# Attention scores of a hybrid decoder layer: fp32 products replaced by three fp32r products of split operands

## The chip, the cores and the metric

The kernel runs on one core of one Trainium2 chip. The metric is the time of one execution on the device in microseconds (us); lower is better. Times are medians of several runs. A profiled execution gives the trace, with the start and length of each instruction on each engine: PE is TensorE's products and PEld its weight loads, DVE is VectorE, ACT is ScalarE, POOL is GpSimd and SP issues the DMAs.

## The reference

One layer for 256 positions of width 2048. The input is normed, and one projection feeds three branches of width 1024. Each is gated by a SiLU, projected back to 2048, merged by sigmoid gates, projected once more, normed and added to the input:

```python
h = rms_norm(x, pre_g)
a_u, a_v, a_g, b_x, b_g, x_q, x_g, gate_logits = split(h @ w_in)
y_a = spatial_gating(a_u, a_v, ...) * silu(a_g)          # layer norm of a_v, causal mix of positions
y_b = s5_branch(b_x, ...) * silu(b_g)                     # complex diagonal scan, gelu, then a GLU
y_x = memory_cross_attention(x_q, rms_norm(mem), ...) * silu(x_g)
out = sum(sigmoid(gate_logits[n]) * (y_n @ w_branch[n])) @ w_out
return x + rms_norm(out, post_g)
```

The change touches the cross-attention: 4 heads of width 256, 256 queries, 256 memory keys.

```python
k = (mem_n @ w_k).reshape(bsz, n_mem, XA_HEADS, XA_HEAD_DIM)
scores = einsum('bshd,bmhd->bhsm', qh, k) * (XA_HEAD_DIM ** -0.5)
p = softmax(scores, axis=-1)
o = einsum('bhsm,bmhd->bshd', p, v)
```

## The kernel before, in words

All matrices are fp32. The large products are made as fp32r products of a high and a low part: `split_to` (L91) has ScalarE round a tile to fp32r (L92, the high part) and VectorE subtract that from the tile (L93, the low part). For a weight tile w and an input x, the kernel adds w_hi x_hi, w_hi x_lo and w_lo x_hi. `cm_mm` (L173 to L177) does so with channels on the partitions, by a product of 512 columns for w_hi (both parts of x side by side) and one of 256 for w_lo; `tm_mm` (L180 to L182) does it with positions on the partitions, by three products of 512 columns.

Weights come from HBM in tiles of 1 MB (`raw`, three buffers). Each is split in two halves, each half into one of four `hl` buffers. The products of one half are called a block here: eight pairs of `cm_mm` or twelve products of `tm_mm`, 2.6 us on TensorE either way. A split of weights may start when TensorE has finished the block four before it.

The stages follow each other on TensorE: `w_bx` (S5 input), `w_xq` (queries), `wk` and `wv` (keys and values of the memory), `w_xg`, gates and projection of the attention branch (`merge(2)`), `w_av`, `w_ag` (beside it the layer norm of a_v, L819 on), `w_au`, `merge(0)`, `w_bg`, the gates of branch B (`sgB`), the GLU of the S5 branch (`yg` against `glu`), its projection, `w_out`.

TensorE's instructions run in the order in which the program is written. Those of the other engines are put in order by a scheduler, by priority and by when their inputs should be there; splits of weights are given priority.

Small work is put between the blocks by hand-written generators. After each block `pump` is called with a credit (`rate`). It first steps each generator in the list `bg[2]` to its next `yield None`, and takes the numbers that they yield from the credit; what is left goes to the S5 work, `s5_main`, which stops when the credit is spent. The S5 work has 32 steps: a product `bu` (L560), multiplies by tables E, two scans (L599), multiplies again, sums `s`. After every fourth step one readout `y` (L624, eight products) follows, then a gelu (`s5_gelu`, L639 on): VectorE adds into U (L374), ScalarE squares (L643), VectorE does two steps (L368, L371), ScalarE takes a sigmoid (L647), VectorE multiplies into U (L371). The result is split (L92, L93) into `yg` (H2, H3), input of the GLU; its last part, the eighth, comes from the last readout.

Attention is four generators of this kind, `attn(h)`, started together at `w_xg`: head h first waits 4h blocks, then makes its scores (L711: two query blocks by two halves of the head, fp32, 256 columns each) in the single PSUM buffer `misc`, then the softmax, then transposes (L732) in a block each. `attn_out(h)` follows in `merge(2)`. The queries lie in slot X0 (`qT`), the keys in M0 (`kT`), the values in M1. Slots H0 to H3 held the normed memory until the end of `wv`; in `w_xg` H0 receives `sx` and H1 the transposed probabilities, and H2 and H3 receive `yX` once attention's output is made.

Of the kernel before, what the change touches and what calls it, by code (L numbers as in the profile page):

```python
# [10 lines left out]
F32R = mybir.dt.float32r  # L11
# [7 lines left out]
P = 128  # L19
# [24 lines left out]
def trunk(ctx: ExitStack, tc: tile.TileContext, I, out):  # L44
    nc = tc.nc
    v, a, g, pe = nc.vector, nc.scalar, nc.gpsimd, nc.tensor
# [18 lines left out]
    def nm(s):  # L65
        n_[0] += 1
        return f"{s}_{n_[0]}"

    def slot(tag, shape, dt=F32):
        return big.tile(shape, dt, tag=tag, name=nm(tag))  # L70

    def small(shape, dt=F32):
        s = nm("sm")
        return const.tile(shape, dt, tag=s, name=s)
# [16 lines left out]
    def split_to(hi, lo, src):  # L91
        a.copy(out=hi, in_=src)  # L92
        v.tensor_tensor(out=lo, in0=src, in1=hi.bitcast(F32), op=ALU.subtract)  # L93
# [38 lines left out]
    def in_order2(z):  # L132
        return z.rearrange("p i (b c) -> p i c b", c=2)
# [518 lines left out]
    qT = slot("X0", [P, 8, T])  # L652
# [16 lines left out]
    kT = slot("M0", [P, 8, T])  # L669
# [35 lines left out]
    def attn(h):  # L705
        for _ in range(4 * h):
            yield None
        sc = miscp.tile([P, 2, T], F32, tag="misc", name=nm("sc"))
        for qb in range(2):
            for c in range(2):  # L710
                pe.matmul(sc[:, qb, :], lhsT=qT[:, 2 * h + c, qb::2], rhs=kT[:, 2 * h + c, :],  # L711
                          start=c == 0, stop=c == 1)
        yield None
        nb = small([P, 2])
        sm = small([P, 2])
        v.tensor_reduce(out=nb, in_=sc, axis=AX.X, op=ALU.max)
        v.tensor_scalar(out=nb, in0=nb, scalar1=-1.0 / 16.0, scalar2=None, op0=ALU.mult)
        p = wk.tile([P, 2, T], F32, tag="w1", name=nm("p"))
        for qb in range(2):
            a.activation(out=p[:, qb, :], in_=sc[:, qb, :], func=AF.Exp, scale=1.0 / 16.0, bias=nb[:, qb:qb + 1],  # L720
                         accum_out=sm[:, qb:qb + 1])
        yield 0.7
        yield None
        v.reciprocal(out=sm, in_=sm)
        for qb in range(2):
            v.tensor_scalar(out=p[:, qb, :], in0=p[:, qb, :], scalar1=sm[:, qb:qb + 1], scalar2=None, op0=ALU.mult)
        yield 0.6
        yield None
        tp = miscp.tile([P, 2, T], F32, tag="misc", name=nm("tp"))
        for mb in range(2):  # L730
            for qb in range(2):
                pe.transpose(tp[:, mb, qb * P:(qb + 1) * P], p[:, qb, mb::2], ident)  # L732
        yield None
        a.copy(out=pT[:, h], in_=tp)

    def attn_out(h):
        for _ in range(h):
            yield None
        po = miscp.tile([P, 2, T], F32, tag="misc", name=nm("po"))
        for c in range(2):  # L740
            for mb in range(2):
                pe.matmul(po[:, c, :], lhsT=vv[:, mb, (2 * h + c) * P:(2 * h + c + 1) * P], rhs=pT[:, h, mb, :],
                          start=mb == 0, stop=mb == 1)
        yield None
        o = wk.tile([P, 2, T], F32, tag="w1", name=nm("o"))
        t = o.rearrange("p i (c b) -> p i c b", c=2)
        d = in_order2(sx[:, 2 * h:2 * h + 2, :])
        a.activation(out=t, in_=d, func=AF.Sigmoid)
        v.tensor_tensor(out=d, in0=po.rearrange("p i (c b) -> p i c b", c=2), in1=d, op=ALU.mult)
        yield 0.6  # L750
        v.tensor_tensor(out=t, in0=d, in1=t, op=ALU.mult)
        yield 0.6
        t = o
        d = yX[h // 2][:, 2 * (h % 2):2 * (h % 2) + 2]
        split_to(d[:, :, 0], d[:, :, 1], t)
        yield 1.2
# [3 lines left out]

    rate["cm"] = RT[2]
    bg[2].extend(attn(h) for h in range(4))
    cm_pairs(I["w_xg"], 8, xhl, evac_xg)
    bg[2].extend(attn_out(h) for h in range(4))

    mg = None
# [19 lines left out]
    def csl(c):  # L786
        return slice(c * 512, (c + 1) * 512)
# [116 lines left out]
    for bp in range(4):  # L904
# [9 lines left out]
        b = slice(2 * bp, 2 * bp + 2)  # L914
        v.tensor_tensor(out=t, in0=t, in1=u[:, b, :], op=ALU.mult)
        v.tensor_tensor(out=t, in0=t, in1=sb[:, b, :], op=ALU.mult)
        for i in range(2):
            d = yB[2 * bp + i]
# [25 lines left out]
    for c in range(4):  # L944
# [3 lines left out]
        for tb in range(2):  # L948
            d = sgB[tb][:, csl(c)]
# [68 lines left out]
    for tb in range(2):  # L1018
# [3 lines left out]
        c = slice(tb, tb + 1)  # L1022
# [107 lines left out]
```

## Time and profile before

| | |
|---|---|
| median of 3 runs | 917.3 us (917.0 to 917.46) |
| span of the profiled execution, first to last instruction | 915.4 us |
| instructions | 12965 |
| granted TensorE clock, mean | 0.998 of full |
| DMA read from HBM | 190.39 MB, 210 GB/s over the span |
| busy in 180 to 190 us (first scores) | PE 10.00, DVE 8.02, ACT 7.60 of 10 us |
| busy in 210 to 220 us | PE 10.00, DVE 6.59, ACT 4.37 of 10 us |

The time of a run is a little above the span, which leaves out what lies ahead of the first and behind the last instruction. In a row of the order of time the columns are: start in us from the span's start, length in us, engine, line, operation, output<-inputs, partitions x elements, xcount where equal rows are merged, and in brackets how long the engine had stood idle and what ended that. In a row of waits: who waited for whom, us in total, times, the longest. In a row of one line's instructions, three lengths in ns are the least, the median and the greatest. A product's length includes its way through the array, so neighbours overlap: what it costs is the distance between starts.

### The profile page before, as it was taken

To read this page: it belongs to the slowest core of one execution; us is meant where nothing else is said; L and a number is where in the kernel's file an instruction comes from. 1 tells how busy PE (TensorE), PEld (TensorE's weight loads), DVE (VectorE), ACT (ScalarE), POOL (GpSimd) and SP (SyncE) were. 2 spreads that over 40 slices of the span, in tenths; PEclk is the share of its full clock that TensorE was granted. 3 is DMA by queue.
4 is the path that set the end of the run, shared out by engine and by line. 5 is a ranking of instruction groups with operands and counts; after the bars stand their busy time and mean duration, and the time that the engine had idled before them with its cause. 6 is when DMAs were issued, how large, how long until landed. Compare 5 with 4: busy or idle time off the path is not lost. (4 is left out here: it accounts for less than half of the span.)

```text
span 915.4 us, 12965 instructions
## 1 busy us (share of the span) xinstructions
PE 902.2 (99%) x4864; PEld 797.8 (87%) x4864; DVE 779.5 (85%) x1329; ACT 535.0 (58%) x866; POOL 22.2 (2%) x46
## 2 busy tenths in 40 slices
PE   8999999999999999999999999999999999999996
PEld 6999898899888888888899888888988888998896
DVE  7899957986789999999877999999998977876554
ACT  7576655665456576565545656756655646544452
POOL 1000000000000000000000000000000000000000
PEclk9999999999999999999999999999999999999999
DMA  9888655556355556555655555555665456657542
GB/s 343 325 304 301 218 214 194 190 192 228 138 190 193 197 197 241 214 184 200 247 184 184 190 185 193 203 193 198 227 216 213 174 208 228 218 185 276 192 176 92
DMA packets 30175, 193.33 MB, mean 211 GB/s; under 512 B 3744, under 2 KB 4128, under 8 KB 8352
## 3 DMA queue, kind: packets, MB, share of 16 engines
q1 hardware_dynamic: 28000, 186.08, 56.9%
q0 software_dynamic: 1536, 4.20, 1.4%
q10 hardware_dynamic: 576, 2.23, 0.6%
q8 instruction: 38, 0.62, 0.3%
q14 instruction: 25, 0.20, 0.1%
HBM read 190.39 MB, written 2.10 MB: 210 GB/s over the span
## 5 line engine op out<-in xcount | busy, mean ns | idle before, releaser
L93 DVE TENSOR_TENSOR hl<-raw,hl 128x1024 fp32r<-128x1024 f32 x319 | 388.5, 1221 | 97.3 <-ACT hl L92 93.8
L92 ACT CAST hl<-raw 128x1024 fp32r<-128x1024 f32 x319 | 330.2, 1045 | 182.5 <-PE acc L182 109.8
L175 PE MATMUL acc<-x,hl 128*128 128x512 f32 x736 | 241.1, 382 | 0.2 <-DVE x L169 0.2
L174 PE MATMUL acc<-x,hl 128*128 128x256 f32 x690 | 189.7, 275 | 2.1 <-DVE hl L93 1.8
L181 PE MATMUL acc<-hl,x 128*128 128x512 f32 x448 | 170.4, 380 | 1.1 <-DVE hl L93 1.0
L180 PE MATMUL acc<-hl,x 128*128 128x512 f32 x448 | 171.3, 382 | 0.0
L182 PE MATMUL acc<-hl,x 128*128 128x512 f32 x448 | 169.8, 379 | 0.0
L175 PEld LDWEIGHTS acc<-x,hl 128*128 128x128 f32 x736 | 136.7, 189 | 17.5 <-ACT hl L92 0.7
L174 PEld LDWEIGHTS acc<-x,hl 128*128 128x128 f32 x690 | 132.3, 192 | 4.9 <-DVE hl L93 3.6
L181 PEld LDWEIGHTS acc<-hl,x 128*128 128x128 f32 x448 | 84.7, 189 | 14.2 <-DVE hl L93 3.0
L180 PEld LDWEIGHTS acc<-hl,x 128*128 128x128 f32 x448 | 84.7, 189 | 13.8 <-issue 2.5
L182 PEld LDWEIGHTS acc<-hl,x 128*128 128x128 f32 x448 | 84.7, 189 | 11.8
L180 PE MATMUL acc<-hl,H 128*128 128x512 f32 (+1 forms) x224 | 83.6, 373 | 0.0
L181 PE MATMUL acc<-hl,H 128*128 128x512 f32 (+1 forms) x224 | 83.2, 372 | 0.0
L182 PE MATMUL acc<-hl,H 128*128 128x512 f32 (+1 forms) x224 | 83.2, 372 | 0.0
L175 PE MATMUL acc<-H,hl 128*128 128x512 f32 x192 | 62.8, 383 | 0.1
L174 PE MATMUL acc<-H,hl 128*128 128x256 f32 x176 | 48.3, 275 | 0.4 <-ACT H L92 0.4
L180 PEld LDWEIGHTS acc<-hl,H 128*128 128x128 f32 x224 | 42.4, 189 | 5.6 <-issue 0.4
L182 PEld LDWEIGHTS acc<-hl,H 128*128 128x128 f32 x224 | 42.4, 189 | 5.6
L181 PEld LDWEIGHTS acc<-hl,H 128*128 128x128 f32 x224 | 42.4, 189 | 5.3
L371 DVE TENSOR_TENSOR p<-p,E 128x512 f32<-128x512 f32 x64 | 44.1, 689 | 1.0
L599 DVE TENSOR_TENSOR_SCAN p<-s5r,p 128x256 f32<-128x256 f32 x64 | 42.5, 683 | 0.9
(248 smaller groups left out, 1166.4 us busy)
## 6 DMA issues: line engine op xcount, KB each, us to landing
raw<-w_gate SPq DMA_DIRECT2D x48, 1024.0 KB, 4.7
raw<-w_br SPq DMA_DIRECT2D x24, 1024.0 KB, 4.7
raw<-w_out SPq DMA_DIRECT2D x16, 1024.0 KB, 4.8
raw<-w_xq SPq DMA_DIRECT2D x8, 1024.0 KB, 5.0
raw<-wk SPq DMA_DIRECT2D x8, 1024.0 KB, 4.7
raw<-wv SPq DMA_DIRECT2D x8, 1024.0 KB, 4.8
raw<-w_xg SPq DMA_DIRECT2D x8, 1024.0 KB, 4.7
raw<-w_av SPq DMA_DIRECT2D x8, 1024.0 KB, 4.8
```

The source lines that it names most:

```text
L92: a.copy(out=hi, in_=src)
L93: v.tensor_tensor(out=lo, in0=src, in1=hi.bitcast(F32), op=ALU.subtract)
L174: pe.matmul(ps[:, 0:T], lhsT=wl, rhs=hl.moving(0), start=False, stop=False)
L175: pe.matmul(ps, lhsT=wh, rhs=hl.moving_both(), start=first, stop=last)
L180: pe.matmul(ps, lhsT=hl.stationary(0, tb), rhs=two(wh), start=first, stop=False)
L181: pe.matmul(ps, lhsT=hl.stationary(0, tb), rhs=two(wl), start=False, stop=False)
L182: pe.matmul(ps, lhsT=hl.stationary(1, tb), rhs=two(wh), start=False, stop=last)
L371: v.tensor_tensor(out=o, in0=i0, in1=i1, op=op)
L599: v.tensor_tensor_scan(out=p2[:, ri], data0=rb, data1=p1[:, ri], initial=0.0, op0=ALU.mult, op1=ALU.add)
```

## The change

Each head now first splits its queries and its keys into high and low parts, in the same way as weights, in slot H2 (heads 0 and 2) or H3 (heads 1 and 3). The split also puts even and odd columns apart. Each split yields 0.6 of credit, as other work of VectorE does. Two blocks later the scores are made: for each query block and each half of the head the products high x high, high x low and low x high, each of 256 columns, twelve a head for the four of before. As the rest of attention is then two blocks later, `attn_out` waits two blocks longer. Lines behind the scores have numbers greater by 8 in the changed kernel.

```diff
     def attn(h):
         for _ in range(4 * h):
             yield None
+        qk = slot(f"H{2 + h % 2}", [P, 2, 2, 2, 2, P], F32R)
+        for i, f in enumerate((qT, kT)):
+            d = f[:, 2 * h:2 * h + 2].rearrange("p k (b c) -> p k c b", c=2)
+            split_to(qk[:, i, :, :, 0], qk[:, i, :, :, 1], d)
+            yield 0.6
+        yield None
+        yield None
         sc = miscp.tile([P, 2, T], F32, tag="misc", name=nm("sc"))
         for qb in range(2):
             for c in range(2):
-                pe.matmul(sc[:, qb, :], lhsT=qT[:, 2 * h + c, qb::2], rhs=kT[:, 2 * h + c, :],
-                          start=c == 0, stop=c == 1)
+                q_, k_ = qk[:, 0, c], Pairs(qk[:, 1, c])
+                for i, (x_, y_) in enumerate(((0, 0), (0, 1), (1, 0))):
+                    pe.matmul(sc[:, qb, :], lhsT=q_[:, qb, x_], rhs=k_.moving(y_), start=c + i == 0, stop=c == 1 and i == 2)
         yield None
...
     def attn_out(h):
-        for _ in range(h):
+        for _ in range(h + 2):
             yield None
```

Three places show how the order moves. VectorE before, from the weights of block 2 of `w_xg` (hl_1912) to those of block 3 (hl_1940); p and E are an S5 step's:

```order
L93 TENSOR_TENSOR hl_1912<-raw_1884,hl_1912 128x1024
L599 SCALAR_TENSOR_TENSOR p_190_1870<-s5r,p_189_1869 128x256
L374 SCALAR_TENSOR_TENSOR E_1867<-E_1867,pwr,t_2349 128x64 x2
L371 TENSOR_TENSOR p_189_1869<-p_190_1870,E_1766 128x512
L371 TENSOR_TENSOR p_190_1870<-p_190_1870,E_1766 128x512
L93 TENSOR_TENSOR hl_1940<-raw_1938,hl_1940 128x1024
```

The same place now (hl_1910, hl_1931; H_199 is head 0's tile of splits, X its queries, M its keys):

```order
L93 TENSOR_TENSOR hl_1910<-raw_1884,hl_1910 128x1024
L93 TENSOR_TENSOR H_199_1905<-X_38_548,H_199_1905 128x4x128
L93 TENSOR_TENSOR H_199_1905<-M_80_1017,H_199_1905 128x4x128
L599 SCALAR_TENSOR_TENSOR p_190_1870<-s5r,p_189_1869 128x256
L374 SCALAR_TENSOR_TENSOR E_1867<-E_1867,pwr,t_2572 128x64
L93 TENSOR_TENSOR hl_1931<-raw_1929,hl_1931 128x1024
L374 SCALAR_TENSOR_TENSOR E_1867<-E_1867,pwr,t_2572 128x64
L371 TENSOR_TENSOR p_189_1869<-p_190_1870,E_1766 128x512
L371 TENSOR_TENSOR p_190_1870<-p_190_1870,E_1766 128x512
```

The head's two subtractions have come in, and the S5 multiplies and one step of E have moved behind block 3's weights. VectorE before, at the start of the layer norm beside `w_ag` (BN_STATS; hl_4031 and hl_4061 are weights of blocks 4 and 5 of `w_ag`). The scan L599 and p are an S5 step's, whose two multiplies by E and two sums s stand further down:

```order
L93 TENSOR_TENSOR hl_4031<-raw_4008,hl_4031 128x1024
L827 BN_STATS sm_3967<-H_443_3539 128x6
L827 BN_STATS sm_4123<-H_443_3539 128x6
L829 BN_AGGR sm_3968<-sm_3967 128x2
L599 SCALAR_TENSOR_TENSOR p_567_4444<-s5r,p_566_4443 128x256
L831 TENSOR_SCALAR sm_3972<-sm_3968 128x1
L93 TENSOR_TENSOR hl_4061<-raw_4059,hl_4061 128x1024
```

The same place now (hl_4033 and hl_4054 are the weights of blocks 3 and 4):

```order
L93 TENSOR_TENSOR hl_4033<-raw_4031,hl_4033 128x1024
L371 TENSOR_TENSOR p_502_3962<-p_502_3962,E_3858 128x512
L371 TENSOR_TENSOR s_4845<-p_501_3961,p_502_3962 128x256 x2
L93 TENSOR_TENSOR hl_4054<-raw_4031,hl_4054 128x1024
L835 BN_STATS sm_3990<-H_439_3563 128x6
L835 BN_STATS sm_4146<-H_439_3563 128x6
L837 BN_AGGR sm_3991<-sm_3990 128x2
```

The S5 step's last multiply and its sums now stand ahead of the statistics. ScalarE before, around the gelu of the last readout (L643, L647; H_836 and H_837 are the last gates of `sgB`, H_945 the GLU's eighth input):

```order
L92 CAST hl_7191<-raw_7189 128x1024
L643 ACTIVATE gl_7087<-U_129 128x256
L647 ACTIVATE gl_7087<-gl_7087 128x256
L92 CAST hl_7210<-raw_7189 128x1024
L897 ACTIVATE H_836_6357<-acc_6939,sm_1065 128x512
L897 ACTIVATE H_837_6358<-acc_6939,sm_1065 128x512
L92 CAST H_945_7094<-U_129 128x2x128
```

The same place now:

```order
L92 CAST hl_7262<-raw_7241 128x1024
L905 ACTIVATE H_835_6387<-acc_6980,sm_1065 128x512
L905 ACTIVATE H_836_6388<-acc_6980,sm_1065 128x512
L643 ACTIVATE gl_7156<-U_129 128x256
L647 ACTIVATE gl_7156<-gl_7156 128x256
L92 CAST H_950_7163<-U_129 128x2x128
```

The gates' sigmoids have moved ahead of the gelu. At the same place on TensorE, before, the end of the last readout (y) and the first of twelve gate products (x) that stand between it and the GLU:

```order
L624 MATMUL y_7077<-s_6978,cb 32x256
L624 MATMUL y_7077<-s_7057,cb 32x256
L180 MATMUL acc_6939<-hl_7097,x_127 128x512
L181 MATMUL acc_6939<-hl_7097,x_127 128x512
L182 MATMUL acc_6939<-hl_7097,x_127 128x512
```

Now the readout's end and the GLU's first products (H_949 is its input):

```order
L624 MATMUL y_7146<-s_7062,cb 32x256
L624 MATMUL y_7146<-s_7141,cb 32x256
L175 MATMUL acc_7188<-H_949_7162,hl_7191 128x512
L177 MATMUL acc_7188<-H_949_7162,hl_7191 128x256
L174 MATMUL acc_7188<-H_949_7162,hl_7191 128x256
```

The twelve gate products now stand ahead of the readout.

## Prediction

> **What bounds the kernel now.** I read the page first, then who waited for whom on TensorE, then the order of time around the places that the change touches.
>
> ```profile
> span 915.4 us, 12965 instructions
> PE 902.2 (99%) x4864; PEld 797.8 (87%) x4864; DVE 779.5 (85%) x1329; ACT 535.0 (58%) x866; POOL 22.2 (2%) x46
> ```
>
> TensorE is busy for 99% of the span, so a microsecond taken from its products is a microsecond of the time unless a new wait eats it. Its waits for other engines, summed over the whole execution, are few:
>
> ```profile
> PE acc L174 <- DVE hl L93: 1.8, 3, 1.0
> PE acc L181 <- DVE hl L93: 1.0, 2, 0.6
> PE acc L174 <- ACT H L92: 0.4, 1, 0.4
> ```
>
> The first two are waits for the low half of a weight tile, which VectorE makes (L93); the third is one wait at the GLU, for the S5 branch's last result. So two queues matter besides TensorE: VectorE's, and the chain that ends the S5 work. The span of 915.4 us is the profiled execution's; the median of the runs is 917.3, so 1.9 us lie around the span. I sum against the span and add 1.9.
>
> **Part 1: the scores.** The products of one head in TensorE's order of time:
>
> ```profile
> 178.65 0.27 PE L174 MATMUL acc<-x,hl 128*128 128x256 f32 x1
> 178.76 0.38 PE L175 MATMUL acc<-x,hl 128*128 128x512 f32 x1
> 178.98 1.89 PE L711 MATMUL sc<-M,X 128*128 128x256 f32 x8
> 180.51 0.46 PE L174 MATMUL acc<-x,hl 128*128 128x256 f32 x1
> 180.81 0.38 PE L175 MATMUL acc<-x,hl 128*128 128x512 f32 x1
> ```
>
> The four fp32 products show as eight records. From their first start to the second product behind them is 1.83 us; 0.11 of that is the L174 product's own (178.65 to 178.76), so a head costs 1.72 us. The new form is twelve fp32r products of 256 columns, each with its own weights. The nearest rows are the kernel's last products, which have just that shape:
>
> ```profile
> 902.76 0.28 PE L182 MATMUL oacc<-wh,H 128*128 128x256 f32 x1
> 902.87 0.28 PE L180 MATMUL oacc<-wh,H 128*128 128x256 f32 x1
> ...
> 904.10 0.28 PE L182 MATMUL oacc<-hl,H 128*128 128x256 f32 x1
> ```
>
> Twelve steps take 904.10 - 902.76 = 1.34 us, so a head costs 1.34, and four heads save 4 x (1.72 - 1.34) = 1.52 us. Upper end: steps of 0.109, as from 178.65 to 178.76 where a long product follows, give 1.65. Lower end: the first product behind the group now takes 0.30 instead of 0.11 (180.51 to 180.81); if leaving the new group cost those 0.19 as well, 0.76 would remain.
>
> [...]
>
> **Part 2: the splits, on VectorE and ScalarE.** Per head two casts (ScalarE) and two subtractions (VectorE) of 128x512 with every second column read, eight of each in all. The nearest rows:
>
> ```profile
> L93 DVE TENSOR_TENSOR hl<-H,hl x8: 689/694/697, 13.6 to 20.6; 128x512 fp32r<-128x512 f32 x8
> L93 DVE TENSOR_TENSOR uhl<-U,uhl x8: 793/812/827, 114.1 to 643.8; 128x256 fp32r<-128x256 f32 x8
> L93 DVE TENSOR_TENSOR H<-U,H x8: 426/493/518, 509.1 to 759.5; 128x256 fp32r<-128x256 f32 x8
> ```
>
> A plain one takes 0.69 us; two of the third row's size, which read every second column, 0.85 to 1.04; two of the second row's, which read every fourth, 1.62. I take 0.9: 7.2 us more on VectorE. They are on the path only if they make a weight tile late. The stretch is the first blocks of w_xg (a block is the products of one weight half, 2.6 us). By VectorE's order, shown with the change, the two subtractions of head 0 stand between the weight tiles of blocks 2 and 3; two S5 multiplies and one small step have moved behind the second of these tiles. What they were worth, and when that tile was made and used before:
>
> ```profile
> 177.72 1.41 DVE L371 TENSOR_TENSOR p<-p,E 128x512 f32<-128x512 f32 x2
> 179.04 1.22 DVE L93 TENSOR_TENSOR hl<-raw,hl 128x1024 fp32r<-128x1024 f32 x1
> 183.10 0.60 PE L175 MATMUL acc<-x,hl 128*128 128x512 f32 x2
> ```
>
> Out go 1.41 and about 0.23, in come 1.8: the tile is ready at about 180.4 instead of 180.26. Of the two products at 183.10 the second, 0.22 later, is block 3's first: the lead was 183.32 - 180.26 = 3.1. TensorE now wants the tile earlier, since head 0's scores stand two blocks later: 183.32 - 1.72 = 181.6. The lead shrinks to 1.2 us and covers it, and from block 5 on the S5 work that stood there has moved away. I take 0; without that cover, each microsecond past 1.2 is one of the time. The key and query tiles go to slots whose readers ended with wv, and the scores wait for splits made two blocks ahead: 0.
>
> **Part 3: the S5 branch falls behind.** Each split takes 0.6 of the credit that paces the S5 work, 4.8 in all, so from here on the S5 steps stand about three blocks later. Where VectorE is the late engine, that helps. In the stretch 410 to 445 us (layer norm beside w_ag) the weight loads waited for it:
>
> ```profile
> PEld acc L174 <- DVE hl L93: 1.5, 3, 0.7
> PEld acc L177 <- DVE hl L93: 0.8, 4, 0.2
> PE acc L174 <- DVE hl L93: 0.4, 1, 0.4
> ```
>
> By VectorE's order the scan (L599), the two wide multiplies and both s of an S5 step stood behind the norm's statistics; now that step is done ahead of them.
>
> ```profile
> 415.88 0.64 DVE L599 TENSOR_TENSOR_SCAN p<-s5r,p 128x256 f32<-128x256 f32 x1
> ```
>
> So 0.64 + 1.41 = 2.05 us and the two s leave the queue in which the tiles were late. The rows bound the gain at 2.3 (all that the loads waited) and at 0; I take 1.0, between the products' own 0.4 and 2.3.
>
> **Part 4: the wait at the GLU.** The lag also moves the last S5 readout (y, L624). Before, a block of twelve gate products stood between y and the GLU; now none does. Behind y runs a chain to the GLU's eighth input. TensorE before (L175 at 756.69 is the GLU's first product, 759.52 and 759.98 the two that need that input):
>
> ```profile
> 753.00 1.07 PE L624 MATMUL y<-s,cb 128*32 128x256 f32 x16
> 754.32 0.38 PE L181 MATMUL acc<-hl,x 128*128 128x512 f32 x1
> 756.69 0.38 PE L175 MATMUL acc<-H,hl 128*128 128x512 f32 x1
> 758.77 0.38 PE L175 MATMUL acc<-H,hl 128*128 128x512 f32 x1
> 759.52 0.38 PE L174 MATMUL acc<-H,hl 128*128 128x256 f32 x1 [0.37 <-ACT H L92]
> 759.98 0.70 PE L175 MATMUL acc<-H,hl 128*128 128x512 f32 x2
> ```
>
> ScalarE's and VectorE's part of it:
>
> ```profile
> 753.10 1.04 ACT L92 CAST hl<-raw 128x1024 fp32r<-128x1024 f32 x1 [1.55 <-PE acc L182]
> 754.75 0.55 ACT L643 ACTIVATE gl<-U 128x256 f32<-128x256 f32 x1 [0.60 <-DVE U L374]
> 756.64 0.42 ACT L647 ACTIVATE gl<-gl 128x256 f32<-128x256 f32 x1 [1.34 <-DVE gl L371]
> 756.96 1.03 ACT L92 CAST hl<-raw 128x1024 fp32r<-128x1024 f32 x1
> 757.90 1.26 ACT L897 ACTIVATE H<-acc,sm 128x512 f32<-128x512 f32 x2
> 759.05 0.41 ACT L92 CAST H<-U 128x256 fp32r<-128x256 f32 x1
> ```
> ```profile
> 755.77 0.27 DVE L368 TENSOR_SCALAR gl<-gl 128x256 f32<-128x256 f32 x1
> 757.09 0.48 DVE L371 TENSOR_TENSOR U<-U,gl 128x256 f32<-128x256 f32 x1 [0.48 <-ACT gl L647]
> 759.50 0.43 DVE L93 TENSOR_TENSOR H<-U,H 128x256 fp32r<-128x256 f32 x1 [0.24 <-ACT H L92]
> ```
>
> Let Y be y's start. Before, the last product came at Y + 6.98. Without a wait it would have come 0.22 + 0.11 behind 758.77, at 759.10: the wait was 0.88, and 2.41 is the way from the GLU's start to that product. Now the GLU starts at Y + 1.10 (754.32 less one step of 0.22), so its place without a wait is Y + 3.51. The chain's new length: ScalarE now has the cast of the block before y and the last two gate sigmoids ahead of L643 (before, the sigmoids, L897, stood behind L647). So L643 starts at 0.10 + 0.94 (cast, 756.96 to 757.90) + 1.15 (sigmoids, 757.90 to 759.05) = Y + 2.19 and ends at 2.74; L368 to L647 takes 756.64 - 755.77 = 0.87, to 3.64; to U 0.45, 4.09; to the cast 0.48 + 0.03, 4.60; to H 0.45, 5.05; its 0.43 and 0.05 more give Y + 5.53. The wait is 5.53 - 3.51 = 2.02, that is 1.14 more than before. Bounds: a chain as long as before gives 2.6 more; one without the sigmoids ahead (1.15 shorter) 0.0 more.
>
> **The sum:** 915.4 - 1.52 - 1.0 + 1.14 + 0 = 914.0 of span, with 1.9 around it 915.9.
>
> **The rivals.** *No gain beside the layer norm (0.23):* the tiles are late there all the same, since the whole norm stays in that stretch. 917.3 - 1.52 + 1.14 = 916.9. For it: VectorE carries the same S5 total, only in other places. *The GLU's wait does not grow (0.19):* 1.34 of the chain at 756.64 was a wait for VectorE, which did a weight tile first, and that may fall away; 917.3 - 1.52 - 1.0 = 914.8. Against it: the block that covered the chain is gone by the order. *VectorE makes the weights late in w_xg (0.07), slower:* if a subtraction costs the 1.62 of the every-fourth row, each head puts 1.4 us more on the queue; the lead of 1.2 is gone with head 0 (the point is about 1.5 us for one), and TensorE pays the rest of 4 x 1.4, 4.4 us: 917.3 - 1.52 + 1.14 + 4.4 = 921.3 without the layer norm's gain. Against it: the row that reads as the split does costs half of that. *Weight loads bound the new group (0.03), slower:* twelve loads a head for eight.
>
> ```profile
> L711 PEld LDWEIGHTS sc<-M,X x32: 195/197/200, 178.8 to 218.5; 128*128 128x128 f32 x32
> L182 PEld LDWEIGHTS acc<-hl,x 128*128 128x128 f32 x448 | 84.7, 189 | 11.8
> ```
>
> If a product could start only every 0.189, a head would cost 2.27, 0.55 more than now: 917.3 + 2.2 + 1.14 = 920.6; from 0.144 a step the gain is nil. The rows at 902.76 to 904.10 exclude it as far as they go: the same shape, a load each, 0.11 apart. [...] That fp32r products save nothing at all is excluded by the same rows.
>
> **How the numbers follow.** My forecast has 0.48. Range: the second rival's 914.8 with 0.4 more of the layer norm's gain gives 914.4; the first one's 916.9 with 1.0 more at the GLU gives 917.9. About 0.2%, 1.8 us, is what a measurement of this kernel tells from no change: under 915.5 is faster, over 919.1 slower. Faster gets 0.17 of the second rival and 0.16 of my own case; slower 0.05 and 0.02 of the last two; the rest, 0.60, is within.
>
> **What would show it.** Right: L720 in steps of 0.11, some 1.34 a head; no wait of TensorE in w_xg; smaller waits for hl in the 410 to 445 stretch; a wait of about 2 us at the GLU's eighth input, behind y and two sigmoids. Wrong: steps of 0.14 or more, TensorE waiting for hl between 180 and 200 us, or no wait at the GLU.

## The result and the profile after

The changed kernel takes 921.63 us (median of 5, 921.58 to 923.3), the kernel before on the same chip 917.46: a ratio of 1.0052, 95% interval 1.0041 to 1.0063. It is slower by 4.2 us; I had forecast 915.9, with a range up to 917.9.

The profiled execution is one of the two slower ones (spans 921.5 and 921.6; the other three have 919.9). Its page and the list of what TensorE waited for (us in total, times, the longest):

```profile
span 921.5 us, 13014 instructions
PE 903.6 (98%) x4880; PEld 798.5 (87%) x4880; DVE 782.8 (85%) x1337; ACT 541.9 (59%) x874; POOL 22.6 (2%) x46
```
```profile
PE tp L740 <- DVE p L734: 3.4, 2, 2.8
PE acc L174 <- DVE hl L93: 2.1, 4, 1.1
PE acc L174 <- ACT H L92: 1.4, 1, 1.4
PE wps L245 <- POOL wz L242: 1.4, 1, 1.4
PE po L750 <- DVE H L757: 0.8, 2, 0.4
PE acc L181 <- DVE hl L93: 0.6, 1, 0.6
```

TensorE is busy for only 1.4 us more than before (903.6 against 902.2, partly at a lower clock), and the span is 6.1 longer. Two rows are new: the transposes of the probabilities (tp) wait for p, the scaled probabilities, and attention's output (po) waits for the tile that the multiply L757 has to read out. TensorE around the four heads, by the lines of scores and transposes:

```profile
184.71 1.50 PE L720 MATMUL sc<-H 128*128 128x256 f32 x12
194.68 0.80 PE L740 MATMUL tp<-ident,p 128*128 128x128 f32 x4 [0.60 <-DVE p L734]
197.93 1.50 PE L720 MATMUL sc<-H 128*128 128x256 f32 x12
210.04 1.05 PE L740 MATMUL tp<-ident,p 128*128 128x128 f32 x4 [2.75 <-DVE p L734]
```

Head 0's transposes wait 0.60 us, head 1's 2.75; those of heads 2 and 3 have no bracket and no wait. The cause stands in ScalarE's order of time behind head 1's scores:

```profile
199.47 0.84 ACT L92 CAST H<-X 128x512 fp32r<-128x512 f32 x1 [0.24 <-PE sc L720]
200.21 0.86 ACT L92 CAST H<-M 128x512 fp32r<-128x512 f32 x1
202.12 0.34 ACTq L825 DMA_DIRECT2D X<-sg_ln  x1
202.50 1.05 ACT L92 CAST hl<-raw 128x1024 fp32r<-128x1024 f32 x1 [1.43 <-DVE sm L725]
204.71 1.05 ACT L92 CAST hl<-raw 128x1024 fp32r<-128x1024 f32 x1 [1.16 <-PE acc L175]
205.67 0.58 ACT L230 COPY f<-acc 128x512 f32<-128x512 f32 x1
206.14 0.48 ACT L728 ACTIVATE p<-sc,sm 128x256 f32<-128x256 f32 x1
```

and in VectorE's:

```profile
200.72 0.68 DVE L724 TENSOR_REDUCE sm<-sc 128x2 f32<-128x512 f32 x1
201.32 0.78 DVE L93 TENSOR_TENSOR H<-X,H 128x512 fp32r<-128x512 f32 x1
202.01 0.16 DVE L725 TENSOR_SCALAR sm<-sm 128x2 f32<-128x2 f32 x1
```

Read them as one chain. The casts H<-X and H<-M are head 3's splits: its slot, H3, is head 1's, so they are let go at the very moment head 1's scores end (199.47, released by sc). VectorE puts head 3's subtraction (0.78) between head 1's maximum and its scaling, which is done at 202.17. The exponential (L728) could start then. But ScalarE's next instruction in its queue is the issue of the DMA that loads sg_ln, and behind it two casts of weights, the second of which waits 1.16 us for TensorE to free a buffer. The exponential starts at 206.14, 4.0 us after its input. The end of the chain is VectorE's again:

```profile
207.53 0.15 DVE L732 RECIPROCAL sm<-sm 128x2 f32<-128x2 f32 x1
207.65 0.69 DVE L330 TENSOR_TENSOR H<-f,bc_x 128x512 f32<-128x512 f32 x1
208.41 1.23 DVE L93 TENSOR_TENSOR hl<-raw,hl 128x1024 fp32r<-128x1024 f32 x1
209.55 0.61 DVE L734 TENSOR_SCALAR p<-p,sm 128x256 f32<-128x256 f32 x2
```

A weight tile and one other step stand between the reciprocal and the scaling (L734), which starts 1.9 us after the reciprocal has ended; the transposes, which need it, start at 210.04.

Why is that issue there? Its target is the queries' slot, X0. In the kernel before, X0 is read until the fourth head's scores:

```profile
219.15 0.34 ACTq L817 DMA_DIRECT2D X<-sg_ln  x1
```

Now its last reader is head 3's subtraction of the queries, which ends at 202.10; the issue is ready 17 us earlier, and stands in the middle of head 1's softmax.

**The clock.** Behind the 2.75 us of idle time the granted clock falls, in this execution (columns: stretch, its length, PE busy, number of products, granted clock, DMA share, GB/s):

```profile
206.00:210.00 4.00, 1.29 (x8) 1.00 0.71 279
210.00:214.00 4.00, 3.96 (x15) 0.57 0.75 262
214.00:218.00 4.00, 4.00 (x30) 1.00 0.00 0
```

The trace has 15 records of products in four busy microseconds and 30 in the next four. From 210 to 214 us, by single microseconds, the clock is 0.70, 0.50, 0.50 and 0.59: half of full at the lowest; a mean of 0.57 over 4 us is half clock for (1 - 0.57) x 4 x 2 = 3.44 us. The other three executions, at 919.9, are 1.6 us shorter, which is about what such a stretch costs by an estimate from this row (half of 3.44 is 1.72); that they had none is inferred from this, as only the profiled execution has a trace.

**The rest.** The two products behind head 0's scores, and the waits of the weight loads beside the layer norm (410 to 450 us), 1.5 and 0.8 before:

```profile
186.04 0.28 PE L174 MATMUL acc<-x,hl 128*128 128x256 f32 x1
186.16 0.38 PE L175 MATMUL acc<-x,hl 128*128 128x512 f32 x1
```
```profile
PEld acc L177 <- DVE hl L93: 0.9, 3, 0.5
PEld acc L174 <- DVE hl L93: 0.5, 1, 0.5
```

A head's scores cost 186.16 - 184.71 - 0.12 = 1.33 us instead of 1.72. And the GLU (765.68 and 766.15 are the products that need its eighth input):

```profile
760.69 1.07 PE L624 MATMUL y<-s,cb 128*32 128x256 f32 x16
763.87 0.38 PE L175 MATMUL acc<-H,hl 128*128 128x512 f32 x1
765.68 0.38 PE L174 MATMUL acc<-H,hl 128*128 128x256 f32 x1 [1.43 <-ACT H L92]
766.15 0.70 PE L175 MATMUL acc<-H,hl 128*128 128x512 f32 x2
```

From 763.87 to the last start are 2.28 us, 0.33 of them the steps of 0.22 and 0.11 that belong there: a wait of 1.95.

### The profile page after: what moved, and what is told of

Read it like the earlier page. It is cut to its first block, busy times and chain, and to the rows that moved or that the text cites. A ratio compares the mean times of both kernels' runs of the same rounds, so it can differ in the third digit from the quotient of the medians.

```text
span 921.5 us, 13014 instructions
## 1 busy us (share of the span) xinstructions
PE 903.6 (98%) x4880; PEld 798.5 (87%) x4880; DVE 782.8 (85%) x1337; ACT 541.9 (59%) x874; POOL 22.6 (2%) x46
## 4 chain that ended last, share of the span: by engine, by line
PE 72%; DVE 20%; ACT 4%; issue 3%; DMA 1%; SPq 0%; DVEq 0%; ACTq 0%
PE acc L175 17%; PE acc L180 14%; PE acc L181 14%; PE acc L182 14%; PE acc L174 8%; DVE hl L93 8%; DVE p L371 4%; DVE p L599 2%; ACT hl L92 2%; DVE E L374 1%; DVE s L371 1%; PE bx L175 1%; PE y L624 1%; DMA st<-start 1%; DVE B L531 1%
## 5 line engine op out<-in xcount | busy, mean ns | idle before, releaser
L599 DVE TENSOR_TENSOR_SCAN p<-s5r,p 128x256 f32<-128x256 f32 x64 | 42.2, 683 | 0.7
```

What stands on the lines that cost most here:

```text
L599: v.tensor_tensor_scan(out=p2[:, ri], data0=rb, data1=p1[:, ri], initial=0.0, op0=ALU.mult, op1=ALU.add)
```

## The experiments

Theory A: the loss is head 1's softmax, held up by the place of its steps in ScalarE's and VectorE's queues, and in some executions the clock behind it. Theory B: the splits' work itself, some 6 us on VectorE and 7 on ScalarE, makes the softmax or the weights late wherever it stands. Theory C: the loss is what the lagging S5 branch does at the GLU and after.

**E1, the sg_ln issue moved to GpSimd's queue.**

```diff
-    nc.scalar.dma_start(out=lnr, in_=I["sg_ln"].broadcast_to([P, 2, W]))
+    nc.gpsimd.dma_start(out=lnr, in_=I["sg_ln"].broadcast_to([P, 2, W]))
```

> The changed kernel with one line altered: the DMA that loads sg_ln is issued from GpSimd's queue, not ScalarE's. All else, splits, products and credits, stays. By the order ScalarE then takes head 1's exponential right behind the last splits, not behind the issue and two casts of weights. Theory A (the loss is head 1's exponential queued on ScalarE behind two weight casts that themselves wait for TensorE, and the clock drop behind that idle time): the wait of TensorE for p at head 1's transposes, 2.75 us, falls to 0.5 or less; no stretch at half clock follows; about 918.7 us, 2.5 to 3 below the changed kernel. Theory B (the sheer volume of the splits, some 7 us on VectorE and 7 on ScalarE, makes the chain late wherever it stands): the wait moves to another head or tile, and the time stays within 0.7 us of 921.6. Theory C (the loss is at the GLU and elsewhere behind the lagging S5 branch): the wait goes, but the time stays at about 921.

Measured: 918.16 us against 917.27 of the kernel before, ratio 1.0005 (0.9996 to 1.0014). It is 0.9 us above the kernel before, where the changed kernel was 4.2 above it: 3.3 us of the loss are gone with one line. ScalarE now, and the transposes of head 1:

```profile
202.56 0.47 ACT L728 ACTIVATE p<-sc,sm 128x256 f32<-128x256 f32 x1 [1.13 <-DVE sm L725]
```
```profile
207.49 0.63 PE L740 MATMUL tp<-ident,p 128*128 128x128 f32 x4
```

The exponential waits for its scaled maximum alone, and the transposes for nothing; the scaling of p now follows the reciprocal at once, at 203.81. Head 0's 0.6 us and the GLU's wait are as in the changed kernel. The splits are all still made, so B doesn't hold for head 1, and C can't hold for more than what is left.

**E2, priority for the softmax instead.** The issue stays on ScalarE.

```diff
+        with tc.high_priority(offset=300):
             v.tensor_reduce(out=nb, in_=sc, axis=AX.X, op=ALU.max)
...
+        with tc.high_priority(offset=300):
             v.reciprocal(out=sm, in_=sm)
```

> The changed kernel with the softmax of each head (maximum, scaling, exponentials, reciprocal, scaling) given the scheduler's priority that casts of weights have; the sg_ln issue stays on ScalarE. By the order head 1's exponentials come right behind that issue and ahead of the two weight casts. Theory A: TensorE's wait for p at head 1's transposes falls from 2.75 us to under 1, about 919 us. If only the issue itself held the queue and not the casts behind it, the wait stays above 2. Theory B: weights come late instead (TensorE waits for hl between 190 and 215 us), 921 or more. Theory C: about 921.

Measured: 918.28 us, ratio 1.0011 (1.0002 to 1.002). ScalarE:

```profile
201.78 0.34 ACTq L827 DMA_DIRECT2D X<-sg_ln  x1
202.17 0.47 ACT L729 ACTIVATE p<-sc,sm 128x256 f32<-128x256 f32 x1 [1.41 <-DVE sm L726]
```

The issue is where it was and does no harm: the casts behind it were the hold-up. Two different edits that have only head 1's exponential in common give the same time.

**E3, no credit for the splits.** S5 keeps its old places.

```diff
             split_to(qk[:, i, :, :, 0], qk[:, i, :, :, 1], d)
-            yield 0.6
```

> The changed kernel without the credit of 0.6 that each split takes from the S5 work: the splits are made, but S5 keeps its places of before, and the last readout stands a block ahead of the GLU again. By the order head 1's exponential still stands behind the sg_ln issue and two weight casts. Theory A: head 1's wait of 2.75 us stays (2 to 4), the GLU's wait falls from 2.0 to about 0.9 us, and the gain beside the layer norm is given back; 920.0 to 921.5 us. Theory C (the lag is the loss): about 917. Theory B: VectorE now carries the splits on top of the S5 work in w_xg, TensorE waits for hl there, above 922.

Measured: 930.04 us, ratio 1.0135 (1.0122 to 1.0149). A and C missed it by far; B has the time, but not for its reason, since TensorE doesn't wait for weights. Two rows of TensorE's list, and its clock:

```profile
PE tp L739 <- DVE p L733: 9.3, 2, 6.6
PE acc L174 <- ACT H L92: 0.4, 1, 0.4
```
```profile
194.00:198.00 4.00, 0.00 (x0) 0.78 0.19 33
198.00:202.00 4.00, 2.27 (x9) 0.50 0.57 233
202.00:206.00 4.00, 4.00 (x27) 0.86 0.72 262
```

The GLU's wait is back at 0.4, as A had it, but the waits for p have grown to 9.3 us, 6.6 of them now at head 0, and the clock is at half around it. C falls: with S5 where it was, the kernel is slowest. Whether A or B made it so is asked by the next run.

**E9, no credit, but the softmax in front.** E3 with the edits of E1 and E2.

> The version without the splits' credit, which had 9.3 us of waits at the transposes and took 930.0 us, now with the softmax's priority and with the sg_ln issue on GpSimd. Splits, S5's places and the GLU's order stay as they were in it. Theory A (it is the place of the softmax's steps in the two queues, not the amount of work in them): the waits at the transposes fall from 9.3 us to under 1.5, no half clock, 917 to 918.5 us. Theory B (with S5's work at its old pace VectorE and ScalarE can't hold the splits): the softmax or the weights come late all the same, 922 or more.

Measured: 920.72 us, ratio 1.0038 (1.0024 to 1.0051), between the two expectations. Head 1's wait is gone; head 0's stays:

```profile
PE tp L741 <- DVE p L735: 3.0, 1, 3.0
```

VectorE ahead of it:

```profile
190.13 1.27 DVE L599 TENSOR_TENSOR_SCAN p<-s5r,p 128x256 f32<-128x256 f32 x2
191.32 1.20 DVE L93 TENSOR_TENSOR hl<-raw,hl 128x1024 fp32r<-128x1024 f32 x1
192.44 0.68 DVE L724 TENSOR_REDUCE sm<-sc 128x2 f32<-128x512 f32 x1
193.04 0.73 DVE L93 TENSOR_TENSOR H<-X,H 128x512 fp32r<-128x512 f32 x1
193.69 0.16 DVE L725 TENSOR_SCALAR sm<-sm 128x2 f32<-128x2 f32 x1
193.76 0.68 DVE L93 TENSOR_TENSOR H<-M,H 128x512 fp32r<-128x512 f32 x1
```

Two S5 scans, a weight tile and head 2's two subtractions share the queue with head 0's maximum. So B is half right: at S5's old pace, with the same priority, head 0's softmax is still late, and the credit of 0.6 takes 3.04 us of wait down to 0.6 (E1, E2). That VectorE has no room for it there, and not only a bad order, is argued and not shown: an S5 multiply still stood between head 0's reciprocal and the scaling.

**E4, the arrangement alone.** The kernel before, with the credit and the two blocks of delay, no splits, fp32 scores.

```diff
         for _ in range(4 * h):
             yield None
+        yield 1.2
+        yield None
+        yield None
...
-        for _ in range(h):
+        for _ in range(h + 2):
```

> The kernel before with the change's arrangement alone: each head gives up 1.2 of credit and starts its scores two blocks later, attn_out waits two blocks longer; no splits are made and the scores stay fp32. Theory A: no splits, so the softmax isn't held up (waits at the transposes under 1 us); what is left is the GLU's wait, 1.2 more, less the layer norm's 0.9: 917 to 918.2 us. Theory B: the same. Theory C: 920 to 921.

Measured: 918.44 us, ratio 1.0012 (1.0003 to 1.0021), a little above the range. Its list has 0.2 us for p, none at attention's output and the changed kernel's 1.4 at the GLU. So the wait at the GLU belongs to the arrangement, and the 2.75 at head 1 does not. E1 and E2 are only 0.3 and 0.2 us faster than E4: without head 1's wait, what the fp32r scores save is nearly used up by the waits that come with them.

**E5, fp32 scores at the new places.** The splits are made but not read, so head 3's aren't held back by head 1's scores any more.

```diff
-                    pe.matmul(sc[:, qb, :], lhsT=q_[:, qb, x_], rhs=k_.moving(y_), start=c + i == 0, stop=c == 1 and i == 2)
+                pe.matmul(sc[:, qb, :], lhsT=qT[:, 2 * h + c, qb::2], rhs=kT[:, 2 * h + c, :], start=c == 0, stop=c == 1)
```

> The changed kernel with its four fp32 score products put back at the changed kernel's places. The splits of queries and keys are still made, but nothing reads them, so the splits of head 3 no longer wait for head 1's scores; by the order head 1's exponential isn't behind the weight casts. Theory A: no wait of more than 1 us at head 1's transposes and no half clock, so the time is that of the version with the sg_ln issue on GpSimd, 918.2, plus the 1.52 that the fp32r scores had saved: 919.3 to 920. Theory B (volume of the splits): the wait stays, 922 to 923.

Measured: 919.05 us, ratio 1.0021 (1.0012 to 1.003). As much casting and subtracting as in the changed kernel, and no wait at head 1: what matters is when the splits are let go and where the issue stands. The time is a little below the range. Each against its own kernel before, E5 is 1.7 us slower and E1 0.9, so fp32 scores cost 0.8 and not 1.5. E5 has no wait at attention's output, where E1 has 0.8; that this is the difference fits, but no run shows it alone.

**E6, S5 catches up ahead of the GLU.**

```diff
+    rate["tm"] = RT[6] + 0.3
     sgB = [slot("H0", [P, D]), slot("H1", [P, D])]
```

> The changed kernel with one line added: in the stage of gates ahead of the GLU the S5 work gets 0.3 more credit a block, so that by the order the last readout stands four blocks ahead of the GLU and not right at it. Theory A: the GLU's wait (1.4 us in the list of waits, 1.59 from start to start) goes, and head 1's wait stays: 919.5 to 920, which is 1.6 to 2.1 below the changed kernel. Theory C (the lag of S5 is the whole loss): 917 or less.

Measured: 920.56 us, ratio 1.0035 (1.0022 to 1.0048). The list has no wait at the GLU any more and the same 3.5 us for p. The time is above the range: the loss against the kernel before went from 4.2 to 3.2 us, as the executions spread from 919.4 to 921.6. The profiled one, with a granted clock of 1.00 from 194 to 218 us, has a span of 918.3, 1.6 below the 919.9 of the changed kernel's shorter ones. So Part 4's term is real, and small beside head 1.

**E7, all of it, and E8, the control.** E7 has E1's and E2's edits, E6's line, and priority for the multiply at attention's output; E8 is the kernel before with E6's line at 0.15.

> The changed kernel with every wait that the trace shows treated: the sg_ln issue on GpSimd, the softmax and the first multiply behind attention's output given priority on VectorE and ScalarE, and 0.3 more credit a block for S5 in the gates' stage. Theory A: TensorE's waits for p under 0.8 us, none at attention's output, none at the GLU: from 918.2 less 0.8 less 1.6 to 2.0, so 915.3 to 916, faster than the kernel before by 1.5 to 2. Theory B: weights come late for the priority given away, 917.5 or more.

> The kernel before with one line added: 0.15 more credit a block for S5 in the gates' stage, so that by the order the last readout stands four blocks ahead of the GLU; the scores stay as before. It tells what of the last version's gain belongs to S5's pace alone. All theories: the GLU's wait of before (0.4 in the list of waits, 0.88 by the step from product to product) goes, 916.4 to 917.1.

Measured: E7 916.51 us, ratio 0.9989 (0.9981 to 0.9998); E8 916.39, ratio 0.9989 (0.998 to 0.9997). Of E8 only the times are used, so that its wait at the GLU went is not shown. E7 is 0.5 above its range: 0.7 us at head 0's transposes and 0.8 at the output were left. And the kernel before gains as much from S5's pace alone.

**E10, two more steps moved.** E7, with the scaling of the maximum on ScalarE and the sigmoid ahead of the output's multiply given priority.

```diff
-            v.tensor_scalar(out=nb, in0=nb, scalar1=-1.0 / 16.0, scalar2=None, op0=ALU.mult)
+            a.activation(out=nb, in_=nb, func=AF.Copy, scale=-1.0 / 16.0)
...
-        a.activation(out=t, in_=d, func=AF.Sigmoid)
         with tc.high_priority(offset=300):
+            a.activation(out=t, in_=d, func=AF.Sigmoid)
```

> The version with all waits treated, 916.5 us, in which 0.7 us of wait at head 0's transposes and 0.8 at attention's output were left. Two more edits: the scaling of the maximum goes from VectorE, where it stands behind one of head 2's subtractions, to ScalarE; and the sigmoids ahead of attention's output get priority on ScalarE. Theory A (what is left comes from the order of the queues too): head 0's wait falls to 0.2 or less and the output's two waits to 0.4 in all, so 915.4 to 915.8 us. Theory B (the splits' work fills the engines there): the waits stay and the time is 916.3 or more.

Measured: 915.59 us against 916.94, ratio 0.9985 (0.9976 to 0.9994): faster than both kernels. Its list and head 0's transposes:

```profile
PE po L752 <- DVE H L760: 0.7, 2, 0.4
```
```profile
193.80 0.80 PE L742 MATMUL tp<-ident,p 128*128 128x128 f32 x4
```

Head 0's wait was head 2's subtraction between the maximum and its scaling, as expected; the output's waits did not move, so the sigmoid wasn't their cause. What is stays open: E4 and E5, with fp32 scores, have none, and the runs with fp32r scores have 0.5 to 0.8 us. The intervals of E8 and E10 overlap: what the fp32r scores add beyond S5's pace is at most some tenths of a per cent, and isn't resolved here.

## Why the prediction was wrong

**Part 1 held.** 1.33 us a head for a predicted 1.34. From start to start that is 1.33 / 12 = 0.111 for each of the twelve products.

**Part 2 failed, and with it the forecast.** The price was about right: subtractions of 0.80 and 0.78 us for 0.9 taken. ScalarE's casts, which its heading names, had no price at all; they took 0.84 and 0.86 us, and ScalarE was busy for 6.9 us more. The failed step is "they are on the path only if they make a weight tile late". I followed the splits to one consumer, the weights, whose lead held; no row shows TensorE waiting for hl there. The other chain in the same queues, maximum to exponential to scaling to transposes, has three blocks, 7.8 us, and was not looked at. The second failed sentence is "the key and query tiles go to slots whose readers ended with wv, and the scores wait for splits made two blocks ahead: 0". That is true of heads 0 and 1. Heads 2 and 3 take over the slots of heads 0 and 1, so their splits start just when these heads' softmax does. And the splits end the queries' life early, which pulled the sg_ln issue 17 us forward. I had followed VectorE's order in this stretch and not ScalarE's, where that issue and the exponentials stand.

**Part 3 held in its stretch; that it held for the whole is luck.** 1.0 was predicted. From the start of the 144th to that of the 156th weight half the changed kernel takes 32.39 us (409.54 to 441.93) for 33.20 (404.30 to 437.50) before: 0.8. The lag is the cause: E4 has it without the splits and takes 32.43, E3 has the splits without it and takes 33.18. But the lag moved S5 work everywhere behind attention, and the sum had no term for the other stretches. All versions make the same products with weights in the same order, so the time between two of them can be compared (us; the first column is their start in the kernel before):

| from, to | before | changed | E4 | E3 |
|---|---|---|---|---|
| 178.10, 300.16 (attention) | 122.06 | 127.48 | 123.01 | 134.26 |
| 300.16, 404.30 | 104.13 | 103.47 | 103.47 | 103.91 |
| 404.30, 437.50 (layer norm) | 33.20 | 32.39 | 32.43 | 33.18 |
| 437.50, 640.05 | 202.55 | 201.70 | 201.66 | 202.54 |
| 640.05, 752.04 (`w_bg`, `sgB`) | 111.99 | 113.52 | 113.44 | 111.99 |
| 752.04, 762.04 (GLU) | 10.00 | 11.07 | 11.08 | 10.02 |

In the second and fourth rows the change gains 1.5 us more, and in the fifth it loses 1.5; E4 does the same, E3 hardly at all. That the two cancel was not foreseen.

**Part 4 held:** a wait of 2.02 predicted, 1.95 measured; the chain is the one forecast (L643 starts at 762.91 behind the two sigmoids, 2.22 after y, for 2.19 predicted). E6, where the wait is gone, and E4, where the arrangement alone brings it, agree.

**The rivals.** The one with VectorE late had the nearest time, 921.3, and the wrong mechanism: its wait was to be for hl, and the splits' price, 1.62, was to be twice what it is. The weight-load rival falls with the steps of 0.111: twelve loads of 0.188 to 0.192 us pass in a head's 1.33 us, beside the products.

**The sum, by what was measured,** on the two profiled spans: -1.56 for the scores, -0.8 beside the layer norm, +1.1 at the GLU, +3.35 for p (0.60 + 2.75), +0.8 at the output, +1.6 for the clock: +4.5 of 6.1. Of the remaining 1.6, 0.5 was there ahead of the scores in this execution; the table's second, fourth and fifth rows cancel; and about 1.2 more lies between 178 and 300 us. E4 loses 1.0 there without splits or fp32r scores, so the arrangement itself costs most of that. The prediction had no term for it, and no run takes it apart. By the medians, which lie among the shorter executions, the loss is 4.2, and E1 takes 3.3 of it away.

## What to carry to other kernels

Work that hides under a busy engine must be checked against every chain that shares its queue, not only against the tightest one: list what stands between each producer and consumer in the new order, on each engine, with DMA issues. Ask of each reused slot when it now comes free, for that moment is when the next owner's work, and any load waiting for the slot, enters the queues: here head 3's casts at 199.47 us, and the sg_ln issue at 202.12 for 219.15 before. And ask what a wait holds up behind it in its queue: here ScalarE's 1.16 us for a weight buffer stood ahead of the exponential.

## What the runs showed of the hardware

An idle time of TensorE of 2.75 us was followed by half clock in the changed kernel and in E3, and not in E6. In the changed kernel half clock lasted 3.44 us. In E9, behind 3.04 us of idle time:

```profile
194.00:198.00 4.00, 1.43 (x6) 0.84 0.02 4
198.00:202.00 4.00, 4.00 (x22) 0.73 0.73 252
```

(0.16 + 0.27) x 4 x 2 = 3.44 us again, with 0.50 in each microsecond from 197 to 200; and in E3, around 6.57 us at head 0, (0.22 + 0.50 + 0.14) x 4 x 2 = 6.88, twice that, and at head 1, where 2.75 us stood idle, 0.84 and 0.73 as in E9. E6 had the same 2.75 us of idle time and kept its clock:

```profile
210.00:214.00 4.00, 3.52 (x23) 1.00 0.73 256
```

So an idle time of 2.75 us alone does not decide whether half clock follows; what does is left open here. In the changed kernel such a wait cost about 1.6 us beyond itself where half clock followed, by the estimate from the spans of 921.5 and 919.9.
